# Second chunk's recurrence gates placed twelve matmuls earlier in a hybrid RG-LRU and attention encoder block

## The chip, the cores and the metric

The kernel runs on one core of a Trainium2 chip. The metric is the device time of one execution in microseconds (us). Before the change it was 1428.52 us, the median of three runs (1427.59 to 1429.19).

## What is computed

One encoder block over 1024 tokens of width 1024, all in float32. After an RMSNorm the block has two mixers side by side, a gated recurrence (RG-LRU) in both directions and a windowed attention; both are gated, added and projected, and a SwiGLU follows. The change lies in the recurrence:

```python
proj = rmsnorm(x, norm_mix_g) @ w_in
u, g_lru, q, k, v, z = jnp.split(proj, splits, axis=-1)
uc = centred_depthwise_conv(u, conv_w, conv_b)          # width 4
# for each direction, ub = uc in 16 blocks of 64 channels:
r = sigmoid(einsum("bshi,hij->bshj", ub, wa) + ba)
i = sigmoid(einsum("bshi,hij->bshj", ub, wx) + bx)
log_a = -8.0 * r * softplus(-lam)
a, beta = exp(log_a), sqrt(max(-expm1(2.0 * log_a), 0.0))
h = associative_scan(h[t] = a[t] * h[t-1] + beta[t] * (i * uc)[t])
y_a = (h_fwd + h_bwd) * gelu(g_lru)
merged = sigmoid(z_A) * y_a + sigmoid(z_B) * y_b
```

## The kernel before

**Layout.** Channels lie on the 128 partitions and tokens run along the free axis, so a tile of 128 channels is 128 x 1024. The recurrence is worked off in eight such chunks, numbered 0 to 7; the change touches chunk 1, the second.

**Products.** To keep float32 precision, each operand is split into a high part and a rest (`xh` and `xl`, `whi` and `wlo`), and a product is three matmuls per 128-deep step k: hi·hi, lo·hi, hi·lo. A projection of one chunk onto 1024 tokens has two halves (n = 0, 1) of 8 steps, so 48 matmuls of 512 columns. The projections go in a fixed list (`order`): for chunks from 2 on, u, then g (the GELU branch), then za (the gate z_A). `u` is accumulated in the PSUM tile `pu`, g and za in the two buffers of `pa`. The weight splits `whi` and `wlo` are made on GpSimd (lines 124 and 127), a ring of three ahead of the matmuls.

**A chunk of the recurrence** (`lru_chunk`) follows its u product:

- `evac_u` takes u out of PSUM and convolves it: two ScalarE passes (`uc`, line 610) and six VectorE passes (line 615).
- The result is split into `uh` (ScalarE, line 120) and `ul` (VectorE, line 127). These two are queued behind the next evacuation of g or za.
- The gate products `gp` follow, for direction d = 0 and then d = 1, twelve small matmuls each: four `gh` x `uh`, four `gh` x `ul`, four `gl` x `uh`. Each direction fills two PSUM tiles, and there are two buffers of these, so the gates of the second direction wait until ScalarE has read those of the first.
- ScalarE turns them into `r` and `i` (line 680, four passes of 64 x 1024), then `q` (tanh, line 689), `r` (exp, line 697) and `q` (sqrt, line 700), each once per direction. tanh and exp share a function table; GELU (line 624) and sqrt have others, and each switch is an ACT_TABLE_LOAD on ScalarE. The tanh of za (line 632) is a ScalarE pass too.
- VectorE does line 691 on `i`, the clamp of `q` (line 690), lines 703 and 704, the two scans (lines 706 and 708), the sum (709) and the output (713, 714).
- The gate weights of a chunk come in by four DMAs into `graw` (line 650) and are split into `gh` (ScalarE, line 120) and `gl` (GpSimd, line 127); a chunk's coroutine does that when it starts, for a later place in the stream.

**What sets the order.** TensorE's order is written by the program: coroutines are resumed by a counter (`clock`) that each matmul moves on by its columns times 0.00042, so a step k of three matmuls counts 0.645. `lru_chunk` yields a number, and its next part is written as soon as the counter has passed it. The first yield after the split stands between `uh`, `ul` and the gates of direction 0; the second (5.0 in chunk 1) between the two directions. The other engines' order is chosen by a list scheduler that follows the order in which instructions are written, within the priorities and `issue_after` ties given. Every engine then works off its own queue in that order.

Of the kernel before, what the change touches and what calls it, by code (L numbers as in the profile page):

```python
# [19 lines left out]
KD = D // P  # L20
# [11 lines left out]
def kernel(  # L32
# [36 lines left out]
    def kmtile(name, dt):  # L69
        return kmp.tile([P, S], dt, name=name, tag="km")  # L70
# [14 lines left out]
    def mm(o, lhsT, rhs, start, stop):  # L85
        pe.matmul(o, lhsT, rhs, start=start, stop=stop, skip_group_check=True)  # L86
        clock[0] += rhs.shape[-1] * 0.00042
# [30 lines left out]
    def to_hi(eng, o, i):  # L118
        if eng == "act":
            return act.activation(o, i, AF.Copy).ins  # L120
        elif eng == "dve":
            dve.tensor_copy(o, i)
        else:
            pool.tensor_scalar(out=o, in0=i, scalar1=1.0, scalar2=1.0, op0=ALU.mult, op1=ALU.mult)  # L124

    def to_lo(eng, o, i, hi):
        (dve if eng == "dve" else pool).tensor_tensor(out=o, in0=i, in1=hi.bitcast(F32), op=ALU.subtract)  # L127
# [99 lines left out]
    def gb(t, j, d, c):  # L227

        o = 88 + j * 16 + d * KD + c
        return pv[t * HD:(t + 1) * HD, o:o + 1]  # L230
# [409 lines left out]
    def lru_chunk(p2, psB, graw, c):  # L640

        def t2(tag, bufs=1, dt=F32):
            return p2.tile([P, S], dt, name=tag, tag=tag, bufs=bufs)

        for t, w in ((0, lru_wa), (1, lru_wx)):
            for j in range(2):
                o = slice(j * HD, (j + 1) * HD)
                dma(graw[o, :, t * HD:(t + 1) * HD], w[0, :, 2 * c + j].rearrange("d i o -> i d o"))  # L650
        gh = p2.tile([P, 2, P], F32R, name="gh", tag="gh", bufs=2)
        gl = p2.tile([P, 2, P], F32R, name="gl", tag="gl", bufs=2)
        to_hi("act", gh, graw)
        to_lo("pool", gl, graw, gh)
        uc = gs.pop(("uc", c))
        uh = t2("uh", 2, F32R)
        ul = kmtile("ul", F32R)
        before = last_evac[0]
        while last_evac[0] is before:
            yield 0.3  # L660
        with tc.high_priority(), tc.issue_after(last_evac[0]):
            to_hi("act", uh, uc)
            to_lo("dve", ul, uc, uh)
        yield {0: 3.5, 1: 11.0, KD - 1: 7.0}.get(c, 10.0)
        gate = {}
        for d in range(2):
            gp = [psB.tile([P, S], F32, name="gp", tag="gp", bufs=2) for _ in range(2)]
            for g, m, st, sp in ((gh, uh, True, False), (gh, ul, False, False), (gl, uh, False, True)):
                for n in range(2):
                    sl = slice(n * 512, (n + 1) * 512)  # L670
                    for j in range(2):
                        o = slice(j * HD, (j + 1) * HD)
                        mm(gp[j][:, sl], g[o, d, :], m[o, sl], st, sp)
                        clock[0] -= 0.1
            for t in range(2):
                r = t2("ri"[t], 3)
                i = slice(t * HD, (t + 1) * HD)
                for j in range(2):
                    o = slice(j * HD, (j + 1) * HD)
                    sig = act.activation(r[o, :], gp[j][i, :], AF.Tanh, bias=gb(t, j, d, c), scale=0.5).ins  # L680
                gate[t, d] = r
            if d == 0:
                yield {0: 6.0, 1: 5.0, KD - 1: 7.5}.get(c, 7.0)
        lru["gates"] += 1
        q = []
        for d in range(2):
            col = slice(d * KD + c, d * KD + c + 1)
            b = t2("q", 3)
            tanh = act.activation(b, gate[0, d], AF.Tanh, bias=sp2[:, col], scale=sp2[:, col]).ins
            dve.tensor_scalar(out=b, in0=b, scalar1=0.0, scalar2=None, op0=ALU.max)  # L690
            dve.scalar_tensor_tensor(out=gate[1, d], in0=gate[1, d], scalar=1.0, in1=uc, op0=ALU.add, op1=ALU.mult)
            q.append(b)
        with tc.high_priority(), tc.issue_after(sig), tc.issue_after(tanh):
            for d in range(2):
                a = gate[0, d]
                col = slice(d * KD + c, d * KD + c + 1)
                exp = act.activation(a, a, AF.Exp, bias=spm4[:, col], scale=spm4[:, col]).ins
        with tc.issue_after(exp):
            for d in range(2):
                act.activation(q[d], q[d], AF.Sqrt)  # L700
        for d in range(2):
            a, i = gate[0, d], gate[1, d]
            dve.scalar_tensor_tensor(out=q[d], in0=a, scalar=1.0, in1=q[d], op0=ALU.add, op1=ALU.mult)
            dve.tensor_tensor(out=i, in0=i, in1=q[d], op=ALU.mult)
            if d == 0:
                dve.tensor_tensor_scan(q[d], a, i, 0.0, ALU.mult, ALU.add)
            else:
                dve.tensor_tensor_scan(q[d][:, ::-1], a[:, ::-1], i[:, ::-1], 0.0, ALU.mult, ALU.add)
        dve.tensor_tensor(out=q[0], in0=q[0], in1=q[1], op=ALU.add)
        while ("ga", c) not in gs:  # L710
            yield 0.5
        g = gs.pop(("ga", c))
        dve.tensor_tensor(out=g, in0=g, in1=q[0], op=ALU.mult)
        dve.scalar_tensor_tensor(out=mB[c], in0=g, scalar=0.5, in1=mB[c], op0=ALU.mult, op1=ALU.add)
        lru["done"] += 1
# [6 lines left out]
    def mixers():  # L722
# [27 lines left out]
        def u_halves(c):  # L750
            ps = env[0][1].tile([P, S], F32, name="pu", tag="pu", bufs=1)
            for n in range(2):
                sl = slice(n * 512, (n + 1) * 512)
                yield from token_product(("u", c), sl, xh, xl, ps[:, sl])
            gs["u", c] = ps
            evac_u(c)
            spawn(lru_chunk(*env[0], c))
# [614 lines left out]
```

## Time and profile before

| | |
|---|---|
| runs | 1428.52 us median (1427.59 to 1429.19) |
| the profiled execution | 1428.95 us, of which its span is 1427.1 us |
| granted TensorE clock | 0.996 |
| TensorE (PE) busy | 1390.8 us, 97% of the span |
| VectorE (DVE) busy | 942.7 us, 66% |
| ScalarE (ACT) busy | 723.5 us, 51% |
| GpSimd (POOL) busy | 583.4 us, 41% |

In the views below, times are us from the start of the span. A timeline row gives start, duration, engine, line, operation, output and inputs, and in brackets the idle time of the engine just before and what ended it. A row with x4 is four instructions merged. A waits row gives the total, the number of times and the longest. In a table by windows, each engine has its busy time, and PEclk is the granted TensorE clock. The recurrence lies between 405 and 690 us.

### The profile page before, as it was taken

How to read it: one execution, taken by the hardware profiler on the slowest of the kernel's cores; microseconds unless marked ns; L12 is line 12 of the kernel's file. 1: busy time of each engine (PE TensorE's matmuls, PEld its weight loads, DVE VectorE, ACT ScalarE, POOL GpSimd, SP SyncE). 2: the span in 40 equal slices, each digit the busy share in tenths (PEclk: the TensorE clock that was granted, in tenths of full speed). 3: DMA queues.
4: the chain of work that ended last, by engine and by line, in shares of the span. 5: the costliest groups of instructions: out<-in, count | busy, mean ns of one | idle time of the engine just before them, and what ended most of it. 6: DMA issues, size and time to landing. Idle time of an engine off the chain costs nothing.

```text
span 1427.1 us, 18489 instructions
## 1 busy us (share of the span) xinstructions
PE 1390.8 (97%) x6606; PEld 1148.2 (80%) x6606; DVE 942.7 (66%) x1457; ACT 723.5 (51%) x1293; POOL 583.4 (41%) x522
## 2 busy tenths in 40 slices
PE   7999999999999899999999999999999999999997
PEld 6788888888887677777888878888888888888886
DVE  6357767677535898778967865444445454987886
ACT  6446556566528966669544533332333332544446
POOL 3434454454433425553454334555555562110002
PEclk9999999999999999999999999999999999999999
DMA  5111101110121111111253333333444435957643
GB/s 194 45 45 30 30 16 31 30 31 15 31 56 49 38 44 37 47 43 51 70 176 118 108 108 115 99 110 104 118 118 133 126 109 181 347 176 235 202 138 140
DMA packets 147548, 138.90 MB, mean 97 GB/s; under 512 B 11528, under 2 KB 117120, under 8 KB 147456
## 3 DMA queue, kind: packets, MB, share of 16 engines
q1 hardware_dynamic: 147456, 137.72, 31.1%
q8 instruction: 52, 0.85, 0.3%
q14 instruction: 40, 0.33, 0.1%
HBM read 119.08 MB, written 18.61 MB: 96 GB/s over the span
## 4 chain that ended last, share of the span: by engine, by line
PE 58%; ACT 3%; DVE 3%; issue 1%; DMA 0%; POOL 0%; ACTq 0%
PE wo L86 34%; PE pa L86 18%; PE pu L86 4%; PE gp L86 1%; PE wo L90 1%; DVE xg L855 0%; ACT i L680 0%; DVE wop L127 0%; DVE x L1273 0%; DMA wraw<-in_w_out_dram 0%; DVE ho L1186 0%; ACT x L1296 0%; ACT ho L1186 0%; ACT sg L1277 0%; DVE x L1293 0%
## 5 line engine op out<-in xcount | busy, mean ns | idle before, releaser
L86 PE MATMUL wo<-x,wop 128*128 128x512 f32 x1368 | 320.7, 390 | 2.1 <-DVE u L1042 1.1
L86 PEld LDWEIGHTS wo<-x,wop 128*128 128x128 f32 x1368 | 255.5, 188 | 56.2 <-ACT wop L998 2.7
L86 PE MATMUL pa<-xh,whi 128*128 128x512 f32 (+1 forms) x576 | 227.8, 395 | 1.5 <-ACT gg L624 1.4
L86 PE MATMUL pa<-xl,whi 128*128 128x512 f32 (+1 forms) x576 | 224.9, 390 | 0.9 <-DVE xl L253 0.7
L86 PE MATMUL pa<-xh,wlo 128*128 128x512 f32 (+1 forms) x576 | 223.8, 389 | 0.0
L127 POOL TENSOR_TENSOR wlo<-wraw,whi 128x1024 fp32r<-128x1024 f32 (+1 forms) x60 | 164.6, 2744 | 38.4 <-ACT whi L120 25.1
L86 PE MATMUL wo<-wo,ho 128*128 128x512 f32 x726 | 170.2, 389 | 0.0
L86 PEld LDWEIGHTS wo<-wo,ho 128*128 128x128 f32 x726 | 136.2, 188 | 28.7 <-DVE ho L1186 0.4
L124 POOL TENSOR_SCALAR whi<-wraw 128x1024 fp32r<-128x1024 f32 (+1 forms) x48 | 69.5, 1448 | 206.7 <-PE pa L86 147.9
L86 PEld LDWEIGHTS pa<-xh,wlo 128*128 128x128 f32 x576 | 108.3, 188 | 23.2
L86 PEld LDWEIGHTS pa<-xh,whi 128*128 128x128 f32 x576 | 108.5, 188 | 20.6 <-issue 3.5
L86 PEld LDWEIGHTS pa<-xl,whi 128*128 128x128 f32 x576 | 108.5, 188 | 16.6 <-DVE xl L253 2.1
L86 PE MATMUL pa<-x,wop 128*128 128x512 f32 x480 | 117.3, 391 | 0.0
L519 POOL TENSOR_SCALAR s<-s,es 128x384 f32<-128x384 f32 (+1 forms) x128 | 71.9, 581 | 97.2 <-DVE es L517 68.5
L579 DVE TENSOR_TENSOR pl<-pt,ph 128x384 fp32r<-128x384 f32 (+1 forms) x128 | 66.9, 522 | 60.6 <-ACT ph L578 58.0
L998 ACT ACTIVATE wop<-s 128x512 fp32r<-128x512 f32 x66 | 41.6, 630 | 128.7 <-POOL s L987 69.2
L86 PEld LDWEIGHTS pa<-x,wop 128*128 128x128 f32 x480 | 89.4, 188 | 18.2
L514 ACT ACTIVATE s<-s,nm 128x384 f32<-128x384 f32 (+1 forms) x128 | 74.0, 580 | 40.5 <-DVE nm L511 39.3
L578 ACT ACTIVATE ph<-pt 128x384 fp32r<-128x384 f32 (+1 forms) x128 | 58.6, 458 | 64.3 <-PE pt L90 49.7
L127 DVE TENSOR_TENSOR wop<-s,wop 128x512 fp32r<-128x512 f32 x66 | 53.5, 810 | 49.8 <-ACT wop L998 48.9
L505 DVE CUSTOM_DVE_ANT_0 s<-sp,bias 128x384 f32<-128x384 f32 (+1 forms) x128 | 66.3, 519 | 21.9 <-PE sp L86 20.6
L1279 POOL TENSOR_TENSOR x<-x,x 128x512 f32<-128x512 f32 x8 | 11.8, 1490 | 167.0 <-ACT sg L1277 167.0
(213 smaller groups left out, 2713.6 us busy)
## 6 DMA issues: line engine op xcount, KB each, us to landing
wraw<-in_w_in_dram SPq DMA_DIRECT2D x44, 512.0 KB, 4.0
wq<-in_w_ffn_out_dram SPq DMA_DIRECT2D x88, 256.0 KB, 3.7
wraw<-in_w_ffn_in_dram SPq DMA_DIRECT2D x26, 512.0 KB, 4.0
wup<-in_w_ffn_in_dram SPq DMA_DIRECT2D x22, 512.0 KB, 4.7
hid<-H SPq DMA_DIRECT2D x22, 512.0 KB, 3.2
h<-hid SPq DMA_DIRECT2D x44, 256.0 KB, 5.4
s<-in_w_ffn_out_dram SPq DMA_DIRECT2D x66, 128.0 KB, 2.2
wraw<-in_w_out_dram SPq DMA_DIRECT2D x16, 512.0 KB, 3.7
```

What stands on the lines that cost most here:

```text
L86: pe.matmul(o, lhsT, rhs, start=start, stop=stop, skip_group_check=True)
L90: pe.transpose(o, i, ident)
L124: pool.tensor_scalar(out=o, in0=i, scalar1=1.0, scalar2=1.0, op0=ALU.mult, op1=ALU.mult)
L127: (dve if eng == "dve" else pool).tensor_tensor(out=o, in0=i, in1=hi.bitcast(F32), op=ALU.subtract)
L505: dve.tensor_tensor_reduce(out=s[:, :n], in0=sp[:, :n], in1=bias[:, off:off + n], scale=1.0, scalar=-3.0e38, op0=ALU.add, op1=ALU.max, acc ...
L514: act.activation(s[:, :n], s[:, :n], AF.Exp, bias=nm[:, j:j + 1], accum_out=sm[:, j:j + 1])
L519: pool.tensor_scalar(out=s[:, :n], in0=s[:, :n], scalar1=es[:, j:j + 1], scalar2=1.0, op0=ALU.mult, op1=ALU.mult)
L578: act.activation(ph[:, o:o + n], pt[:, :n], AF.Copy)
L579: dve.tensor_tensor(out=pl[:, o:o + n], in0=pt[:, :n], in1=ph[:, o:o + n].bitcast(F32), op=ALU.subtract)
L998: act.activation(t[:, lo4], src, AF.Copy)
L1279: pool.tensor_tensor(out=x1[t][:, lo4], in0=x1[t][:, lo4], in1=gfin[:, lo4], op=ALU.mult)
```

## The change

In `lru_chunk` the first yield of chunk 1 becomes 9.0 instead of 11.0:

```diff
         with tc.high_priority(), tc.issue_after(last_evac[0]):
             to_hi("act", uh, uc)
             to_lo("dve", ul, uc, uh)
-        yield {0: 3.5, 1: 11.0, KD - 1: 7.0}.get(c, 10.0)
+        yield {0: 3.5, 1: 9.0, KD - 1: 7.0}.get(c, 10.0)
         gate = {}
         for d in range(2):
```

No instruction's work changes. Chunk 1's part of the program is written earlier, and so the order changes on five queues. On TensorE, in the product of chunk 2's u (`pu`), the gates of direction 0 of chunk 1 (`gp`) stand as follows (`xh_101` is step k = 6 of a half, `xh_102` step 7):

```order
 L86 MATMUL pu<-xl_109,whi 128x512
 L86 MATMUL pu<-xh_101,wlo 128x512
+L86 MATMUL gp<-uh,gh 128x512 x4
+L86 MATMUL gp<-ul,gh 128x512 x4
+L86 MATMUL gp<-uh,gl 128x512 x4
 L86 MATMUL pu<-xh_102,whi 128x512
 L86 MATMUL pu<-xl_110,whi 128x512
```

They stood behind step 2 of the second half and now stand behind step 6 of the first, four steps or twelve matmuls of 512 columns earlier. The gates of direction 1 move up by the same twelve, from behind step 2 of chunk 2's g to behind step 6 of the second half of its u.

On ScalarE, at the gates of chunk 1, the first two rows are direction 0, `uc` is the evacuation of chunk 2's u, and `gh` the split of a later chunk's gate weights:

```order
 L680 ACTIVATE r<-gp,pv 64x1024 x2
 L680 ACTIVATE i<-gp,pv 64x1024 x2
+L689 ACTIVATE q<-r,sp_86 128x1024
+L120 ACTIVATE gh<-graw 128x256
+L680 ACTIVATE r<-gp,pv 64x1024
 L610 ACTIVATE uc<-pu,pv 128x512 x2
-L689 ACTIVATE q<-r,sp_86 128x1024
-L120 ACTIVATE gh<-graw 128x256
-L680 ACTIVATE r<-gp,pv 64x1024 x2
-L680 ACTIVATE i<-gp,pv 64x1024 x2
+L680 ACTIVATE r<-gp,pv 64x1024
+L680 ACTIVATE i<-gp,pv 64x1024 x2
```

The evacuation of chunk 2's u now stands behind chunk 1's first tanh, the `gh` split and the first `r` of direction 1. Chunk 1's second tanh and its first exp, which the piece no longer shows, follow these rows and stand ahead of the GELU of chunk 2.

Further down ScalarE's queue come the second half of chunk 2's GELU (`gg`), chunk 1's second exp (`r`) and its sqrt (`q`), and chunk 2's za (`sA`):

```order
 L624 ACT_TABLE_LOAD
 L624 ACTIVATE gg<-pa 128x512
-L697 ACT_TABLE_LOAD
-L697 ACTIVATE r<-r,spm_87 128x1024
 L700 ACT_TABLE_LOAD
-L700 ACTIVATE q<-q 128x1024
+L700 ACTIVATE q<-q 128x1024 x2
 L632 ACT_TABLE_LOAD
 L632 ACTIVATE sA<-pa,hbg 128x512
-L700 ACT_TABLE_LOAD
-L700 ACTIVATE q<-q 128x1024
-L680 ACT_TABLE_LOAD
```

Three table loads go: one exp is ahead of the GELU and needs none, and the two sqrt stand together. The rows behind are the `r` and `i` of chunk 2.

On VectorE chunk 1's first clamp (690) moves ahead of chunk 2's convolution (615) and its second ahead of the last 691 and the split `ul`, and the pairs of 703 and 704 stand together. On GpSimd `gl` of a later chunk moves ahead of the weight split of chunk 3's u. On the DMA queue the four `graw` loads of the chunk after that move ahead of one `wraw` load.

## The prediction

> **What bounds the kernel now.** I read the page first, then the waits of TensorE in the stretch of the recurrence, then the timeline around each wait.
>
> ```profile
> span 1427.1 us, 18489 instructions
> PE 1390.8 (97%) x6606; PEld 1148.2 (80%) x6606; DVE 942.7 (66%) x1457; ACT 723.5 (51%) x1293; POOL 583.4 (41%) x522
> ```
>
> ```profile
> PE gp L86 <- ACT i L680: 6.2, 4, 4.4
> PE pa L86 <- ACT gg L624: 1.4, 1, 1.4
> ```
>
> TensorE is busy 97% of the span, so only what it waits for can be won. In the recurrence it waits twice for long: once for a GELU, once 4.4 us for the `i` passes. The timeline puts both in chunk 2, the chunk behind the one that is moved:
>
> ```profile
> 483.19 0.39 PE L86 MATMUL pa<-xh,wlo 128*128 128x512 f32 x1
> 485.02 0.50 PE L86 MATMUL pa<-xh,whi 128*128 128x512 f32 x1 [1.44 <-ACT gg L624]
> ...
> 494.90 0.39 PE L86 MATMUL pu<-xh,wlo 128*128 128x512 f32 x1
> 499.73 0.79 PE L86 MATMUL gp<-uh,gh 64*128 64x512 f32 x1 [4.44 <-ACT i L680]
> 500.86 1.22 PE L86 MATMUL gp<-uh,gh 64*128 64x512 f32 x3 [0.34 <-ACT i L680]
> 505.12 0.39 PE L86 MATMUL pu<-xh,whi 128*128 128x512 f32 x1
> ```
>
> The same passage without a wait is that of chunk 1's direction 0:
>
> ```profile
> 458.04 0.39 PE L86 MATMUL pu<-xh,whi 128*128 128x512 f32 x1
> 459.40 0.39 PE L86 MATMUL pu<-xh,whi 128*128 128x512 f32 x1
> 460.17 0.73 PE L86 MATMUL gp<-uh,gh 64*128 64x512 f32 x4
> 460.74 0.63 PE L86 MATMUL gp<-ul,gh 64*128 64x512 f32 x4
> 461.76 0.50 PE L86 MATMUL pu<-xh,whi 128*128 128x512 f32 x1
> 462.56 0.40 PE L86 MATMUL pu<-xh,whi 128*128 128x512 f32 x1
> 467.42 0.73 PE L86 MATMUL gp<-uh,gh 64*128 64x512 f32 x4
> ```
>
> A step of three matmuls takes (459.40 - 458.04) / 2 = 0.68 us, one matmul 0.23. From the last matmul before the gates (459.40 + 0.45 = 459.85) to the second step behind them (462.56) it is 2.71 us. In chunk 2 the same stretch, 494.90 to 505.12, takes 10.22: 7.5 us are lost there. About 5.5 of it is waiting. The rest is a slow restart: from 500.86 to 505.12 it is 4.26 us, where 2.39 less one matmul (2.25) is usual, so 2.0. The clock shows why:
>
> ```profile
> 485.10:494.40 9.30, 9.30 (x45) 7.18 (x46) 4.41 (x3) 9.18 (x9) 1.88 (x2) 1.00 0.01 3
> 499.70:506.00 6.30, 5.93 (x19) 4.00 (x20) 6.23 (x5) 5.25 (x6) 1.49 (x1) 0.57 0.19 56
> ```
>
> Behind the 4.44 us wait the granted clock (the third number from the end) was 0.57; behind the 1.44 us wait it stayed 1.00. The GELU wait cost 485.02 - 483.19 - 0.23 = 1.6. What could be won here is 7.5 + 1.6 = 9.1 us.
>
> **Term 1: the moved gates meet their own operand, +1.6 us.** Four steps earlier, direction 0 starts at 460.17 - 4 x 0.68 = 457.45, and its second group, the first that reads `ul`, 0.57 later at 458.02.
>
> ```profile
> 454.11 3.25 POOL L127 TENSOR_TENSOR wlo<-wraw,whi 128x1024 fp32r<-128x1024 f32 x1
> 455.02 3.42 DVE L703 SCALAR_TENSOR_TENSOR q<-r,q 128x1024 f32<-128x1024 f32 x1
> 458.37 1.21 DVE L127 TENSOR_TENSOR ul<-uc,uh 128x1024 fp32r<-128x1024 f32 x1
> ```
>
> `ul` is ready at 458.37 + 1.21 = 459.58, and nothing ahead of it moves. TensorE, which never waited there, now waits 1.6 us, and everything queued behind waits with it. So the move is 2.7 us on paper and 1.1 in effect. Bounds: 1.6, and 3.6 if the clock falls as after the 4.44 wait. I take 1.6, because the nearest row is the 1.44 wait with the clock at 1.00.
>
> `ul` is late because line 703 took 3.42 us beside GpSimd's `wlo`; it ended 1.1 us behind that one's end (457.36), as if it had waited for it. I use this below: of a GpSimd pass and a VectorE pass with two SBUF inputs, one holds up the other.
>
> **Term 2: chunk 2's two losses, -9.1 us, of which 0.3 stays.** ScalarE decides. Its rows before:
>
> ```profile
> 461.87 2.25 ACT L680 ACTIVATE r<-gp,pv 64x1024 f32<-64x1024 f32 x2 [4.26 <-PE gp L86]
> 464.14 2.25 ACT L680 ACTIVATE i<-gp,pv 64x1024 f32<-64x1024 f32 x2
> 466.42 1.45 ACT L610 ACTIVATE uc<-pu,pv 128x512 f32<-128x512 f32 x2
> 467.76 1.24 ACT L689 ACTIVATE q<-r,sp 128x1024 f32<-128x1024 f32 x1
> 478.30 1.06 ACT L120 ACTIVATE uh<-uc 128x1024 fp32r<-128x1024 f32 x1 [2.68 <-DVE uc L615]
> 484.37 0.60 ACT L624 ACTIVATE gg<-pa 128x512 f32<-128x512 f32 x1
> 494.29 1.28 ACT L680 ACT_TABLE_LOAD   x1
> 498.56 2.24 ACT L680 ACTIVATE i<-gp,pv 64x1024 f32<-64x1024 f32 x2
> ```
>
> I follow the new queue with these durations. Direction 0's `r` starts 2.7 - 1.6 = 1.1 earlier, at 460.8, and its four passes end at 465.3. TensorE reaches direction 1 at 467.42 - 2.72 + 1.6 = 466.3, so it does not wait there. Then tanh to 466.5. `gh` and the first `r` of direction 1 wait for TensorE (466.3 + 1.59 = 467.9); `r` ends about 469.4, `uc` 470.8 (467.87 before), the other `r` and two `i` 474.2, tanh 475.4, exp (as long) 476.7, a table load and a GELU half 478.6, a microsecond before TensorE wants its bank.
>
> Next is `uh`, which waits for chunk 2's convolution on VectorE:
>
> ```profile
> 474.24 4.03 DVE L615 SCALAR_TENSOR_TENSOR uc<-pu,pv,uc 128x510 f32<-128x510 f32 x6
> ```
>
> It can't start before 470.8. Chunk 1's clamp now stands ahead of it, and GpSimd's split of chunk 3's u weights, pushed behind `gl`, falls beside that: I put the start at 475.7, between 470.8 and 479.2 (one more GpSimd pair of 3.5 us, rows below), near the old 474.24. It ends at 479.7. `uh` 480.8; load, exp, load, GELU half (1.28 + 1.24 + 1.28 + 0.60) 485.2. TensorE wants that bank at 483.42 + 1.6 = 485.0, so some 0.3 us of wait stays instead of 1.6. Behind it: load, two sqrt (1.06 each, as `uh`), load, `sA` (0.6) to 490.5, then `r` and `i` of chunk 2, 4.5, to 495.0. TensorE wants direction 1 of chunk 2 at 495.13 - 1.6 + 1.6 + 0.3 = 495.4. The 4.44 us wait and its slow restart are gone, with 0.4 us to spare. Three loads less, 3.8 us, and one exp taken out from behind the second GELU half make most of the 5.8 us by which `i` ends sooner (500.80 before). The Trainium skill, "ScalarE: Activation LUTs", section "What ACT_TABLE_LOAD costs", gives 2.66 us for a switch, its drain counted; three would be 8.0, the 0.3 us would go and the sum would be 0.3 better. The trace disagrees: the load of 494.29 takes 1.28 and the queue goes on at once.
>
> **Term 3: VectorE has less slack in chunk 3, +1.2 us.**
>
> ```profile
> 489.93 1.22 DVE L703 SCALAR_TENSOR_TENSOR q<-r,q 128x1024 f32<-128x1024 f32 x1 [5.24 <-ACT q L700]
> 510.42 0.68 DVE L690 TENSOR_SCALAR q<-q 128x1024 f32<-128x1024 f32 x1
> 513.90 3.40 DVE L703 SCALAR_TENSOR_TENSOR q<-r,q 128x1024 f32<-128x1024 f32 x1 [2.80 <-ACT q L700]
> 526.55 3.41 DVE L127 TENSOR_TENSOR ul<-uc,uh 128x1024 fp32r<-128x1024 f32 x1
> ```
>
> ```profile
> 512.67 1.06 POOL L124 TENSOR_SCALAR whi<-wraw 128x1024 fp32r<-128x1024 f32 x1 [7.26 <-PE pu L86]
> 513.82 2.40 POOL L127 TENSOR_TENSOR wlo<-wraw,whi 128x1024 fp32r<-128x1024 f32 x1
> ```
>
> ```profile
> 530.31 0.63 PE L86 MATMUL gp<-ul,gh 64*128 64x512 f32 x4
> ```
>
> Chunk 3's `ul` ended at 529.96, only 0.35 before it was read. From 489.93 to 511.10 VectorE was busy or held up, 21.2 us. Now it starts there at 487.6 (sqrt done), 2.3 earlier, while TensorE is 7.2 earlier; and the GpSimd pair of 512.67 (3.5 us), released by TensorE, now falls into this stretch: 487.6 + 21.2 + 3.5 = 512.3. From 511.10 to 529.96 it was 18.9, of it 2.8 idle and twice 2.2 held up: 11.7 is left, so `ul` is ready near 524.0 to 524.3. TensorE wants it at 530.31 - 9.1 + 1.6 + 0.3 = 523.1. I take 1.2 us, between 0 (the pair finds a gap) and 3.6 (a second `wlo` gets ahead, 2.4).
>
> **What costs nothing.** `graw` goes ahead of one `wraw`:
>
> ```profile
> 472.12 1.25 SPq L650 DMA_DIRECT2D graw<-in_lru_wa_dram  x2
> ```
>
> ```profile
> wraw<-in_w_in_dram SPq DMA_DIRECT2D x44, 512.0 KB, 4.0
> ```
>
> Four issues of 0.63 behind `gl` (done near 469.4) let `wraw` go at 472 and land at 476; its split waits for the end of chunk 2's g, about 479.6. If that cover were gone, each us late is one of chunk 3's g weights, wanted 25 us later. The pair that `gl` now precedes is wanted at 492.5 and ends near 475.
>
> **The sum.** -9.1 + 1.6 + 0.3 + 1.2 = -6.0 us. The profiled execution took 1428.95 us (span 1427.1, 1.9 around it), so 1422.9; it lies 0.4 above the median of 1428.52, so the median should be 1422.5. Behind chunk 3 nothing is moved, and TensorE simply runs 6 us earlier. What a measurement of this kernel can tell from no change is about 0.2%, 2.9 us.
>
> **The rivals.**
> *New waits eat the gain (0.09).* Term 3 is at its worse end of 3.6, the clock falls there as behind the 4.44 wait (2.0), and term 2 keeps 2.0: -9.1 + 1.6 + 2.0 + 3.6 + 2.0 = +0.1, 1428.6. For it: VectorE is full from 489.93 on. Against: both terms must come out near their worse ends.
> *The change does little (0.05).* The gates can't pass `ul`; if ScalarE's new order saved nothing and only the 1.1 us went through, both waits shrink by 1.1 and 1.6 is added: 1428.5 - 2.2 + 1.6 = 1427.9. Against: the three loads are gone from the queue.
> *Slower (0.08).* Chunk 2's convolution is held behind two GpSimd pairs, since `uc` is now evacuated 3 us later and the weight split later too. Both GELU halves and chunk 2's gates are queued behind `uh`. Each us that the convolution ends after 479.7 is a us of TensorE's wait for the GELU half; with a wait like the 4.44 one the clock falls too (2.0). It loses all at a delay of 4.0 (4.0 + 2.0 + 0.3 + 1.6 + 1.2 = 9.1); with 6.9 for two pairs the time is 1422.5 + 6.9 + 2.0 = 1431.4. Against: one of the pairs is over by 475. The point at which the clock falls lies between waits of 1.44 and 4.44 in this trace. The Trainium skill, "TensorE: Matmul & The Clock Gate", section "What's actually happening", puts it at an idle window of about 3.4 us; by that this rival's break-even has its 2.0, and rival one's 3.6 as well.
>
> **Chances.** Forecast 0.78, the rivals 0.09, 0.05 and 0.08. The forecast is faster by over 0.2%, the first two rivals are no change, the third is slower. Range: with terms 2 and 3 at nothing, 9.1 - 1.6 = 7.5 are won, 1421.0, and half a us is added for the spread of the runs. With term 2 at its worse end (0.3 + 3.5 of wait) 9.1 - 1.6 - 3.8 - 1.2 = 2.5 are won, 1426.0; with term 3 at its worse end 3.6, 1424.9. The forecast alone would leave out 0.22, so the range reaches on to the second rival: 1420.5 to 1428.0.
>
> **What would show it.** Right: a new TensorE wait of `gp` for VectorE's `ul` near 458 of about 1.5 us at clock 1.00; no wait of 4 us for `i` near 495; at most half a us for the GELU near 485; a wait of 0 to 3.6 for `ul` near 523. Wrong: a convolution of chunk 2 that starts after 479, or any wait over 3 us in the recurrence.

## The result, and the profile after

With the change the kernel takes 1421.05 us (median of four runs, 1420.54 to 1421.23), beside 1428.05 for the kernel before in its four runs. The two medians give a ratio of 0.9951; the ratio on record is 0.9945, with a 95% interval of 0.9932 to 0.9958, and the ratios further down are those on record too. The forecast was 1422.5, faster by 6.0; by the medians it is faster by 7.0.

The span and busy lines of the page after. Against before the span is 7.8 us shorter, TensorE is busy 2.3 us less, and ScalarE has three instructions less:

```profile
span 1419.3 us, 18488 instructions
PE 1388.5 (98%) x6606; PEld 1147.9 (81%) x6606; DVE 939.4 (66%) x1457; ACT 720.1 (51%) x1290; POOL 584.3 (41%) x522
```

TensorE's waits of the change in the stretch of the recurrence (total, times, longest). The GELU line is gone, the 4.4 us wait for `i` too, and `ul` is new; the two small waits for `i` that are left are in chunk 7, where before had them as well:

```profile
PE gp L86 <- DVE ul L127: 2.2, 2, 1.4
PE gp L86 <- ACT i L680: 1.4, 2, 0.8
```

The two waits for `ul` on the change's TensorE timeline, in chunk 1 (459.06) and chunk 3 (523.15), and between them direction 1 of chunk 2 (494.67), where before waited 4.44 us and came back at a granted clock of 0.57:

```profile
456.90 0.73 PE L86 MATMUL gp<-uh,gh 64*128 64x512 f32 x4
459.06 0.73 PE L86 MATMUL gp<-ul,gh 64*128 64x512 f32 x4 [1.43 <-DVE ul L127]
...
460.18 0.50 PE L86 MATMUL pu<-xh,whi 128*128 128x512 f32 x1
...
494.67 0.73 PE L86 MATMUL gp<-uh,gh 64*128 64x512 f32 x4
...
521.64 0.73 PE L86 MATMUL gp<-uh,gh 64*128 64x512 f32 x4
523.15 0.73 PE L86 MATMUL gp<-ul,gh 64*128 64x512 f32 x4 [0.78 <-DVE ul L127]
```

The theory of the cause is read off one queue, and E5 tests it. ScalarE in the change, from the split `uh` of chunk 2 on:

```profile
478.63 1.06 ACT L120 ACTIVATE uh<-uc 128x1024 fp32r<-128x1024 f32 x1 [0.85 <-DVE uc L615]
483.57 0.60 ACT L624 ACTIVATE gg<-pa 128x512 f32<-128x512 f32 x1
484.19 1.28 ACT L700 ACT_TABLE_LOAD   x1
485.48 2.01 ACT L700 ACTIVATE q<-q 128x1024 f32<-128x1024 f32 x2
489.39 2.24 ACT L680 ACTIVATE r<-gp,pv 64x1024 f32<-64x1024 f32 x2
491.65 2.25 ACT L680 ACTIVATE i<-gp,pv 64x1024 f32<-64x1024 f32 x2
```

The same stretch of ScalarE before, with the passes that the change takes out of it:

```profile
479.27 1.23 ACT L689 ACTIVATE q<-r,sp 128x1024 f32<-128x1024 f32 x1
480.51 1.28 ACT L697 ACT_TABLE_LOAD   x1
481.81 1.25 ACT L697 ACTIVATE r<-r,spm 128x1024 f32<-128x1024 f32 x1
...
491.92 1.28 ACT L700 ACT_TABLE_LOAD   x1
493.21 1.06 ACT L700 ACTIVATE q<-q 128x1024 f32<-128x1024 f32 x1
...
497.85 0.69 ACT L632 ACTIVATE sA<-pa,hbg 128x512 f32<-128x512 f32 x1
```

From the end of `uh` to the end of `i` it was 500.80 - 479.36 = 21.4 us before and is 493.90 - 479.69 = 14.2 in the change. The 7.2 us are three table loads that are gone (3.8), one exp (1.2) and one tanh (1.2) that are now done while ScalarE used to wait for the convolution, and half of `sA` (0.7) that now comes behind `i`: 7.0 before rounding, and a rest of 0.2. (The third load is that of 494.29, shown in the prediction.)

**How far a single time can be trusted.** I measure each version by its stretch as well: from the first gates of chunk 0 to direction 1 of chunk 7, on TensorE. Before:

```profile
426.63 0.73 PE L86 MATMUL gp<-uh,gh 64*128 64x512 f32 x4
...
671.30 0.49 PE L86 MATMUL gp<-uh,gh 64*128 64x512 f32 x1 [0.77 <-ACT i L680]
```

The change:

```profile
426.06 0.74 PE L86 MATMUL gp<-uh,gh 64*128 64x512 f32 x4
...
664.25 0.50 PE L86 MATMUL gp<-uh,gh 64*128 64x512 f32 x1 [0.77 <-ACT i L680]
```

That is 244.67 and 238.19 us, a difference of 6.48. What lies outside the stretch (the execution's time less the stretch) is 1184.28 and 1182.87. A stretch is that of the one profiled execution, a median that of all executions. One of E2's nine executions took 4950.94 us and is left out of E2's ratio.

### The profile page after: what moved, and what is told of

It reads as the page before. It is cut to its first block, busy times and chain, and to the rows that moved or that the text cites. A ratio compares the mean times of both kernels' runs of the same rounds, so it can differ in the third digit from the quotient of the medians.

```text
span 1419.3 us, 18488 instructions
## 1 busy us (share of the span) xinstructions
PE 1388.5 (98%) x6606; PEld 1147.9 (81%) x6606; DVE 939.4 (66%) x1457; ACT 720.1 (51%) x1290; POOL 584.3 (41%) x522
## 4 chain that ended last, share of the span: by engine, by line
PE 81%; DVE 10%; ACT 6%; issue 2%; DMA 1%; POOL 0%; SPq 0%; ACTq 0%; DVEq 0%
PE wo L86 34%; PE pa L86 32%; PE pu L86 4%; PE yp L86 3%; PE sp L86 2%; PE pt L90 2%; PE gp L86 1%; DVE q L703 1%; DVE uc L615 1%; PE wo L90 1%; DVE pl L579 1%; ACT s L514 1%; DVE i L691 0%; DVE q L706 0%; DVE i L704 0%
```

## The experiments

The theory: ScalarE's order pays (one exp and one tanh ahead of chunk 2's GELU, three table loads less), and the moved gates as such only cost, by the wait for `ul`. The rival: the gates' place pays, that is, `r` and `i` of chunk 1 come sooner and all that hangs on them too. Two smaller questions are what a table load costs and whether the wait for `ul` in chunk 3 lies on the path.

Each version ran beside the kernel before, whose median was 1429.09 us beside E1 to E4, 1428.29 beside E5 to E8 and 1428.69 beside E9 to E12. "Steps" are how many steps of three matmuls direction 0 and direction 1 of chunk 1's gates stand sooner than before. Stretch and time are us less (-) or more (+) than before.

| | version | steps | stretch | time | ratio (95%) |
|---|---|---|---|---|---|
| | the change | 4, 4 | -6.48 | -7.0 | 0.9945 (0.9932 to 0.9958) |
| E1 | direction 1 one step | 0, 1 | -5.56 | -5.3 | 0.9960 (0.9947 to 0.9972) |
| E2 | direction 0 alone | 4, 1 | -4.75 | -3.4 | 0.9972 (0.9962 to 0.9982) |
| E3 | direction 1 three steps | 0, 3 | -7.14 | -8.0 | 0.9944 (0.9932 to 0.9957) |
| E4 | one step further | 5, 5 | -4.92 | -5.3 | 0.9968 (0.9956 to 0.9980) |
| E5 | the change, old ScalarE order | 4, 4 | +2.04 | +2.1 | 1.0011 (1.0002 to 1.0020) |
| E6 | two steps | 2, 3 | -6.73 | -7.4 | 0.9946 (0.9934 to 0.9959) |
| E7 | two steps, chunk 2 later | 2, 3 | -6.75 | -6.7 | 0.9947 (0.9935 to 0.9960) |
| E8 | the change again | 4, 4 | -6.47 | -6.6 | 0.9949 (0.9935 to 0.9962) |
| E9 | square roots apart | 4, 4 | -3.16 | -4.3 | 0.9969 (0.9958 to 0.9980) |
| E10 | `ul` read last | 4, 4 | -6.21 | -5.9 | 0.9957 (0.9944 to 0.9969) |
| E11 | E3, chunk 3 two steps later | 0, 3 | -8.18 | -8.8 | 0.9936 (0.9923 to 0.9948) |
| E12 | one step, chunk 3 two steps later | 1, 3 | -8.05 | -8.3 | 0.9941 (0.9927 to 0.9955) |

In the expectations of E1 to E4, E6 and E7 "chunk 2's gates" are those of the moved chunk, which is chunk 1 in this document; the time named with each wait says which one is meant. In that of E8, "chunk 1's first gates" are chunk 0's here. In E2 direction 1 did not quite stay: it came out one step sooner, as in E1.

### E1: direction 1 one step sooner

```diff
-                yield {0: 6.0, 1: 5.0, KD - 1: 7.5}.get(c, 7.0)
+                yield {0: 6.0, 1: 4.4, KD - 1: 7.5}.get(c, 7.0)
```

> Only direction 1 of chunk 2's gates moves, by one step of three matmuls (0.68 us) sooner; direction 0 stays where it was, so no wait for its own low half. ScalarE then has the exp ahead of the GELU in chunk 2, one table load fewer and the square roots still apart. Theory A (it is ScalarE's order that pays, not where the gates stand): the GELU wait of 1.4 us near 485 is gone, the wait for the second input gate near 495 is still there but about 3.5 us instead of 4.4; 1.4 + 0.9 = 2.3 us below before if TensorE still comes back at the lower clock, 4.3 us if it does not (the restart was 2.0). Theory B (it is direction 0's gates being sooner that pays): direction 0 has not moved, so the two waits stay and the time is before's within 1 us.

A single step of direction 1 wins 5.56 of the change's 6.48 us, with direction 0 where it was. The order on ScalarE turned: the second tanh and the first exp now stand ahead of the GELU. The GELU wait is gone, and the long wait, in E1's TensorE timeline, is 1.88 instead of 4.44:

```profile
494.53 0.50 PE L86 MATMUL gp<-uh,gh 64*128 64x512 f32 x1 [1.88 <-ACT i L680]
495.66 0.72 PE L86 MATMUL gp<-uh,gh 64*128 64x512 f32 x3 [0.64 <-ACT i L680]
```

This speaks for the theory and against the rival, and the gain is larger than I had put for the theory (2.3 to 4.3). I had counted the load that goes and too little for what is taken out from behind `uh`, which is a tanh, an exp and a load, 1.23 + 1.25 + 1.28 = 3.8 us. The profiled execution is a favourable one, though: it and one more had a granted clock of 0.999 and took 1421.5 and 1422.0 us, the other three had 0.995 to 0.998 and took 1423.8 to 1424.8. E2 is split in the same way, with 1422.5 and 1423.1 at 0.999 and 1424.9 to 1427.5 at 0.995 to 0.997. By the medians E1 wins 5.3 of some 7.

### E2: direction 0 alone

```diff
-        yield {0: 3.5, 1: 11.0, KD - 1: 7.0}.get(c, 10.0)
+        yield {0: 3.5, 1: 9.0, KD - 1: 7.0}.get(c, 10.0)
...
-                yield {0: 6.0, 1: 5.0, KD - 1: 7.5}.get(c, 7.0)
+                yield {0: 6.0, 1: 7.0, KD - 1: 7.5}.get(c, 7.0)
```

> Only direction 0 of chunk 2's gates moves, by four steps as in the change; direction 1 stays where it was. ScalarE has the exp ahead of the GELU, but the square roots are not paired: one load fewer than before, not three. Theory A (ScalarE's order pays): the wait for the low half near 458 is the change's own, 1.4 us; no GELU wait; the second input gate ends two loads and more later than in the change, near 497, so TensorE waits 1.5 to 2.5 us near 495, at clock 1.00 if that is short enough: 5.0 us below before. Theory B (direction 0's place pays): as the change, 7.0 us below.

From chunk 2's `uh` on, ScalarE's order is that of E1, and direction 0 stands four steps sooner. The waits are 1.45 us for `ul` and 1.55 + 0.64 for `i`; the stretch is 0.8 us worse than E1's. Direction 0's place is not what pays.

### E3: direction 1 alone, three steps

```diff
-                yield {0: 6.0, 1: 5.0, KD - 1: 7.5}.get(c, 7.0)
+                yield {0: 6.0, 1: 3.0, KD - 1: 7.5}.get(c, 7.0)
```

> Only direction 1 of chunk 2's gates moves, three steps (2.0 us) sooner; direction 0 stays. ScalarE's order in chunk 2 is the change's in full (exp ahead of the GELU, square roots paired, three loads fewer). Theory A (ScalarE's order pays): no wait for the low half in chunk 2, both of chunk 3's waits gone as in the change, and in their place direction 1 of chunk 2 waits about 1.0 us for the input gate of direction 0: 7.0 to 7.7 us below before, level with the change or a little better. Theory B (direction 0's place pays): within 2 us of before.

The passes and loads from chunk 1's second tanh to chunk 2's `i` stand as in the change, and direction 0 is untouched. I had expected the change's order in full; it differs in that the evacuation `uc` stands ahead of chunk 1's first tanh, as before, and a `gh` split stands elsewhere. The stretch is 0.7 us better than the change's. E3's TensorE waits in the recurrence show why: no wait for `ul` in chunk 1 (the one left, 0.7, is chunk 3's), and 0.56 more for `i`:

```profile
PE gp L86 <- ACT i L680: 2.0, 3, 0.8
PE gp L86 <- DVE ul L127: 0.7, 1, 0.7
```

The theory holds: the gain is had without moving direction 0 at all.

### E4: one step further

```diff
-        yield {0: 3.5, 1: 11.0, KD - 1: 7.0}.get(c, 10.0)
+        yield {0: 3.5, 1: 8.0, KD - 1: 7.0}.get(c, 10.0)
```

> The change carried one step (0.68 us) further: both directions' gates of chunk 2 stand 5 steps sooner than before instead of 4. ScalarE's order in chunk 3's stretch is the change's. Theory A (ScalarE's order pays, the move itself only costs): the wait for the low half near 458 grows from 1.4 to 2.1 us, nothing else moves: 6.3 us below before, 0.7 slower than the change. Theory B (the sooner the better): 7.5 us or more below before.

The wait for `ul` is 2.12 us, as expected, but 1.6 us of the stretch are lost against the change, not 0.7. E4's timeline and, under it, a window of it (length, PE busy with its count, granted clock, DMA share, GB/s) show that the clock fell:

```profile
459.31 1.22 PE L86 MATMUL gp<-ul,gh 64*128 64x512 f32 x4 [2.12 <-DVE ul L127]
460.33 1.06 PE L86 MATMUL gp<-uh,gl 64*128 64x512 f32 x4
```

```profile
459.20:462.90 3.70, 3.59 (x12) 0.55 0.30 89
```

The step costs 0.7 and the slow stretch some 1.5, and 0.6 comes back in chunk 3, whose wait for `ul` is 0.17 instead of 0.78.

### E5: the gates of the change, ScalarE in the old order

The ties hold chunk 1's second tanh behind chunk 2's `uh`, its second exp behind the second GELU half and its second sqrt behind the first half of `sA` (`nxt()` yields until the next evacuation is written). For it the loops over the exps and square roots are written with the ties inside, and the splits `uh` are recorded in `gs`; the gates are not touched. Ahead of chunk 2's first GELU half ScalarE keeps the change's order, so "old" means from there on.

```diff
+            if (c, d) == (1, 1):
+                while ("uh", 2) not in gs:
+                    yield 0.1
+            with tc.issue_after(gs["uh", 2]) if (c, d) == (1, 1) else nullcontext():
+                tanh = act.activation(b, gate[0, d], AF.Tanh, ...).ins
...
+            if (c, d) == (1, 1):
+                yield from nxt()
+                exp = last_evac[0]
```

> All of the gates stand where the change puts them (four steps sooner, direction 1 eight steps behind direction 0); ScalarE's queue is held in before's order from chunk 2's GELU on (GELU and the high half ahead of the exps, each exp and square root apart, three table loads more than in the change). The computation is the same. Theory A (the gain is ScalarE's order): the change's wait for the low half near 458 stays at 1.4 us, and the wait for the second input gate near 495 comes back at 1.5 to 3.5 us, less than before's 4.4 because direction 1's sigmoids end 1.5 us sooner, with the restart of up to 2 us where it is over 2 us; GELU wait 0 to 0.5. In all 2 to 5.5 us below before, so 1.5 to 5 us above the change. Theory B (the gain is the gates' place): level with the change, 7.0 us below before.

This is the run that decides. With the gates where the change has them and the old order on ScalarE, the kernel is slower than before by 2.1 us, 2.04 by the stretch. E5's TensorE timeline:

```profile
458.34 0.73 PE L86 MATMUL gp<-ul,gh 64*128 64x512 f32 x4 [1.45 <-DVE ul L127]
...
484.63 0.50 PE L86 MATMUL pa<-xh,whi 128*128 128x512 f32 x1 [0.57 <-ACT gg L624]
...
499.33 0.50 PE L86 MATMUL gp<-uh,gh 64*128 64x512 f32 x1 [4.44 <-ACT i L680]
500.47 1.22 PE L86 MATMUL gp<-uh,gh 64*128 64x512 f32 x3 [0.63 <-ACT i L680]
```

The wait for `ul` is paid, the 4.44 us wait is back to the hundredth, and only the GELU wait is shorter. That the long wait is the same is no accident: in both versions the second GELU half releases TensorE last, and from that half's start to the end of `i` ScalarE takes the same time, 500.80 - 484.37 = 16.43 us before and 500.42 - 483.98 = 16.44 here. All 8.5 us between E5 and the change are ScalarE's order, with what follows from it on VectorE, whose queue is the change's until chunk 2's convolution is done. I had left the theory 2 to 5.5 us of gain here, since direction 1's sigmoids end sooner; that was wrong. ScalarE waits at `uh` for chunk 2's convolution all the same:

```profile
467.92 1.43 ACT L610 ACTIVATE uc<-pu,pv 128x512 f32<-128x512 f32 x2
477.91 1.06 ACT L120 ACTIVATE uh<-uc 128x1024 fp32r<-128x1024 f32 x1 [3.25 <-DVE uc L615]
```

Counted from chunk 0's gates (425.33), `uc` is evacuated at 42.6 instead of 39.8 and `uh` starts at 52.6 instead of 51.7. So the sooner gates delay what the long chain really hangs on, by 0.9 us. With the 1.1 us by which the restart behind the long wait is slower than before (last section), that is E5's 2.0.

### E6 and E7: two steps, and a gate further on

```diff
-        yield {0: 3.5, 1: 11.0, KD - 1: 7.0}.get(c, 10.0)
+        yield {0: 3.5, 1: 10.0, KD - 1: 7.0}.get(c, 10.0)
...
-                yield {0: 6.0, 1: 5.0, KD - 1: 7.5}.get(c, 7.0)
+                yield {0: 6.0, 1: 4.2, KD - 1: 7.5}.get(c, 7.0)
```

> Direction 0 of chunk 2's gates moves two steps (1.36 us) instead of four, direction 1 three steps instead of four; ScalarE's order is the change's. Theory A (the order pays, the move costs only what it goes beyond the low half's slack of 1.16 us): wait for the low half near 458 0.2 us instead of 1.4, no wait of direction 1 for the input gate of over 0.4 us, nothing near 485 and 495; chunk 3's wait of 0.8 us stays: 1.5 us below the change, 8.5 below before. Theory B (the sooner the better): 3.5 us below before, half of the change's gain.

The wait for `ul` in chunk 1 is down to the expected 0.2 us (the second group starts 0.81 behind the first instead of 0.57), but of the 1.3 us that this saves only 0.25 shows in the stretch. E6's waits in the recurrence say where the rest went:

```profile
PE gp L86 <- DVE ul L127: 1.0, 1, 1.0
PE pa L86 <- ACT gg L624: 0.5, 1, 0.5
```

TensorE now comes 1.2 us sooner to the GELU, and neither ScalarE nor, behind it, VectorE is sooner by as much: the GELU wait returns with 0.5, and chunk 3's wait for `ul` grows from 0.8 to 1.0. E7 adds `2: 10.6` to the first table and `2: 6.4` to the second:

> The version with two steps, and direction 0 of chunk 3's gates one step (0.68 us) later, direction 1 where it was. If chunk 3's wait for the low half (0.78 us, 0.94 with the slower matmuls behind it) is on TensorE's path like chunk 2's, 0.7 us go: 9.2 us below before, 0.7 below the version with two steps. If what waits there is hidden by a later wait, level with that version.

The expectation doesn't fit the edit. Key 2 is chunk 2, and the wait near 522 is chunk 3's, so the edit left it alone (0.99 us), and the stretch is E6's. E7 says nothing on its question; E11 does.

### E8: the change again

> The change itself once more, for how far one execution differs from another outside the recurrence. If the 0.6 us before the first gates and the 0.8 us behind the last ones are spread of single executions, this profile shows other values there, and the stretch from chunk 1's first gates to chunk 3's second direction is 105.9 us again. If they come from the change, they are 0.6 and 0.8 again. The time 7.0 us below before either way, within 0.7.

The stretch is 238.20 us, as in the first profile to a hundredth, and the part outside it 1421.68 - 238.20 = 1183.5, where it had been 1182.9. Over all the profiled executions it goes from 1182.1 (E11) to 1185.1 (E10). Part of that is the clock: in E4, E5, E7, E8 and E10 it fell to half for 3.4 us right behind the stretch, and from the stretch's end on these took 757.9 to 758.0 us, all others 756.8 to 757.7. The change and E8 are one kernel, and one has this fall and the other not; the last section shows the rows. So the 1.4 us by which before's profiled execution is longer outside the stretch are within the spread of single executions, and what the change does is in the stretch.

### E9: square roots apart

```diff
+            if (c, d) == (1, 1):
+                for _ in range(3):
+                    seen = last_evac[0]
+                    while last_evac[0] is seen:
+                        yield 0.1
+                exp = last_evac[0]
             with tc.issue_after(exp):
                 act.activation(q[d], q[d], AF.Sqrt)
```

> The change with one thing undone on ScalarE: chunk 1's two square roots stand apart again, the second behind the first half of chunk 2's sA, with the two table loads (1.28 us each) that this takes. The first exp stays ahead of the GELU and the gates stand where the change has them. Theory A (ScalarE's order pays, and the loads by their own time): the GELU wait near 485 stays away, the i passes of chunk 2 end 2.6 to 3.2 us later than in the change, of which 0.8 are spare: TensorE waits 1.8 to 2.4 us near 495, 4.4 to 5.2 us below before, and 2 less if the clock falls. If a load cost twice as much as its row shows, the wait would be 4.4 to 5 and the clock would fall: level with before. Theory B (the gates' place pays): 7.0 below before.

The edit lets three evacuations pass, so that chunk 1's second square root comes behind the first half of chunk 2's `sA`. This one undoing costs half the gain: 3.3 us of the stretch. E9's ScalarE rows at the second sqrt and the end of `i`:

```profile
489.62 1.28 ACT L706 ACT_TABLE_LOAD   x1
490.92 1.06 ACT L706 ACTIVATE q<-q 128x1024 f32<-128x1024 f32 x1
492.00 1.28 ACT L680 ACT_TABLE_LOAD   x1
493.29 2.25 ACT L680 ACTIVATE r<-gp,pv 64x1024 f32<-64x1024 f32 x2
...
497.42 1.11 ACT L680 ACTIVATE i<-gp,pv 64x1024 f32<-64x1024 f32 x1
```

Counted from chunk 0's gates, `i` ends at 498.53 - 427.14 = 71.4 instead of 67.8: 3.55 us later, which is two loads (2.56), half of `sA` (0.69), 0.1 for the sqrts that no longer overlap, and 0.2. So a load costs its 1.28 us on this queue. The Trainium skill, "ScalarE: Activation LUTs", section "What ACT_TABLE_LOAD costs", counts a drain of 1.38 us with each; as an estimate from that figure, two loads would have made it 6.3, which the trace doesn't show. TensorE's wait came in two pieces, 0.91 and 1.35, and the clock fell for 3.4 us behind them, so the cost is 3.3.

### E10: `ul` read last

```diff
-            for g, m, st, sp in ((gh, uh, True, False), (gh, ul, False, False), (gl, uh, False, True)):
+            for g, m, st, sp in ((gh, uh, True, False), (gl, uh, False, False), (gh, ul, False, True)):
```

> The change with the three groups of a gate's product in another order, in all chunks: the high half with gh, the high half with gl, then the low half, so that ul is read 0.47 us later. If the wait for the low half is what the moved gates cost, the two waits of 1.4 and 0.8 us shrink by 0.47 each and the time is 0.9 us below the change, 7.9 below before. If VectorE's chain to the low half is itself started by TensorE and nothing is won, level with the change.

A miss: 0.3 us worse than the change by the stretch. Chunk 3's wait shrank as expected, from 0.78 to 0.29. Chunk 1's did not (1.48), because `gh` and with it GpSimd's `gl` came forward. E10's VectorE row, then its GpSimd row:

```profile
458.90 1.75 DVE L127 TENSOR_TENSOR ul<-uc,uh 128x1024 fp32r<-128x1024 f32 x1
```

```profile
458.53 1.03 POOL L127 TENSOR_TENSOR gl<-graw,gh 128x256 fp32r<-128x256 f32 x1 [0.64 <-ACT gh L120]
```

Beside that pass `ul` took 1.75 us, not 1.21, and the half microsecond was gone. Also new is a wait of 1.52 for `i` in chunk 7, 0.77 in the change. That wait is where the gain went: TensorE came to it 0.48 us sooner than in the change, counted from chunk 0's gates, and was released 0.27 later, which is what the stretch is worse by.

### E11 and E12: chunk 3's gates later

E11 is E3 with chunk 3's direction 0 two steps later, and E12 the same with direction 0 of chunk 1 one step sooner (10.4 and 3.6 for chunk 1):

```diff
-        yield {0: 3.5, 1: 11.0, KD - 1: 7.0}.get(c, 10.0)
+        yield {0: 3.5, 1: 11.0, 3: 11.2, KD - 1: 7.0}.get(c, 10.0)
...
-                yield {0: 6.0, 1: 5.0, KD - 1: 7.5}.get(c, 7.0)
+                yield {0: 6.0, 1: 3.0, 3: 5.8, KD - 1: 7.5}.get(c, 7.0)
```

> Direction 0 of chunk 1's gates where before has it, direction 1 three steps sooner (as the version with direction 1 alone), and direction 0 of chunk 3's gates two steps (1.36 us) later, its direction 1 in place. If chunk 3's wait for its low half (0.74 us, 0.9 with what follows) is on TensorE's path, it goes and the time is 0.9 us below the version with direction 1 alone, 9 below before. If not, level with that version.

> Direction 0 of chunk 1's gates one step sooner than before (0.68 us, inside the low half's slack of 1.16), direction 1 three steps, so six behind direction 0; chunk 3's direction 0 two steps later. No wait for a low half in chunk 1 or 3, less of the wait of direction 1 for the input gate than the 1.2 us that the version with direction 1 alone shows there; a GELU wait of up to 0.5 us near 483 may come back as in the version with two steps. 0 to 0.7 us below the version with direction 0 in place, 9 to 9.7 below before.

In E11 the wait for `ul` in chunk 3 is gone, and the stretch is 1.0 us shorter than E3's: that wait was on the path. At 1419.90 us it has the lowest median and the shortest stretch, 1.7 us below the change by the stretch (1.2 and 1.8 below its two medians, with intervals that overlap). In E12 the wait for `i` in chunk 1 is gone as well, but the GELU wait of 0.52 returned as in E6, and it is level with E11.

## Where the prediction was right, and the step that failed

**What bounds it.** Right. The 9.1 us of chunk 2's two losses are what the change could win, and they are gone.

**Term 1, +1.6.** Right. From the gates' first row to the product behind them it is 460.18 - 456.90 = 3.28 us instead of 1.59: +1.69, at clock 1.00. E3 shows that this price isn't needed for the gain.

**Term 2, -9.1 + 0.3.** The mechanism was right, and E5 shows it as ScalarE's order alone; the 0.3 was too much. In the change there is no GELU wait. The second GELU half ended at 484.17, forecast 485.2; 0.6 of this is that chunk 0's gates already stood 0.6 sooner in this execution, and by the other 0.5 the chain ran ahead of the forecast.

This is the step that failed: the start of chunk 2's convolution, which the forecast put at 475.7, a choice between two bounds, and from which it kept 0.3 us of GELU wait. It started at 474.57, or 475.14 if the 0.57 of the execution's own is added. What it names as the cause is there: the clamp ahead of the convolution took 2.89 us beside GpSimd's `wlo`, where without such a pass it takes 0.68. VectorE's rows in the change, then GpSimd's:

```profile
471.76 2.89 DVE L690 TENSOR_SCALAR q<-q 128x1024 f32<-128x1024 f32 x1
474.57 4.03 DVE L615 SCALAR_TENSOR_TENSOR uc<-pu,pv,uc 128x510 f32<-128x510 f32 x6
```

```profile
470.85 3.25 POOL L127 TENSOR_TENSOR wlo<-wraw,whi 128x1024 fp32r<-128x1024 f32 x1
```

The forecast's rule named VectorE passes with two SBUF inputs alone; the clamp has one and was held up too. Its account of why `i` ends sooner also left out the tanh (1.23) taken out from behind `uh`, though its times had it.

**Term 3, +1.2.** Right in kind, and the other term that was sized wrong: 523.15 - 521.64 = 1.51 instead of 0.57, so +0.94. `ul` was ready at 523.09, forecast 524.0 to 524.3, again with 0.6 of it the execution's own. E11 shows that it lay on the path.

**The sum.** -9.1 + 1.69 + 0 + 0.94 = -6.47, and the stretch shows -6.48; an agreement this close is partly luck, since the 9.1 is rounded. The forecast of -6.0 was off by half a microsecond, 0.3 in term 2 and 0.26 in term 3, less 0.09 in term 1. Of the 1.45 us between 1422.5 and 1421.05, this is 0.5; another 0.5 is that before's median, 1428.52 in three runs, is 1428.05 in four; the rest lies outside the stretch, where E8 shows a spread of this size, and its cause is open in part. So half a microsecond of the 7.0 is not shown to be the change's.

**The rivals.** "The change does little" had the waits shrink by 1.1 us each if ScalarE's order saved nothing, for 1427.9. E5 is that case, and it is worse: the long wait did not shrink at all, because both its ends hang on the convolution, by way of `uh` and the GELU half, and not on the sigmoids. The slower rival had that piece right (a later `uc`), but in the change the passes taken out from behind `uh` cover it: `uh` waits 0.85 us where it waited 2.68. "Behind chunk 3 nothing is moved" held: the second directions of chunk 3 and of chunk 7 come 7.04 and 7.05 us sooner.

**The clock.** I had the point at which it falls between waits of 1.44 and 4.44, and used 2.0 us as the price. That frame was wrong; the last section has what the runs show.

## What to carry to other kernels

A number that places work on one engine can pay through the order that it brings about on another: the gates' new place cost 1.7 us, and ScalarE's new order was worth 8.5. Before such a number is tuned, the question is which order is wanted, and then which place brings that order about without passing an operand: here direction 1 alone did it, and direction 0 could stay. And when a large wait goes, the engine that waited arrives sooner everywhere behind it, so the next waits (`ul` in chunk 3, the GELU at two steps) are worth a look of their own.

## What the runs showed of the hardware

**The clock does not fall at a certain length of wait.** One wait of 1.43 us (the change) and two of 1.88 and 0.64 (E1) left it at 1.00. One of 2.12 (E4) and two of 0.91 and 1.35 (E9) brought it to half. Windows of E1 over its two waits and behind them (length, PE busy with its count, granted clock, DMA share, GB/s):

```profile
492.60:496.00 3.40, 0.89 (x5) 1.00 0.01 3
496.00:502.00 6.00, 6.00 (x32) 1.00 0.36 102
```

And of before: here the clock fell in the middle of the wait, 2.9 us after it began, and stayed at 0.50 until 505.1:

```profile
495.30:498.20 2.90, 0.00 (x0) 1.00 0.00 0
498.20:504.80 6.60, 4.73 (x15) 0.50 0.28 79
```

It stayed low for 3.41 us in E4 and E9, and for twice that, 6.83, in before and E5, whose wait was the same 4.44 but where the fall came only at 500.2, when TensorE was already back. So the price of such a wait is a matter of when it falls, not of its length alone: the second 4.44 us wait cost 1.1 us more than the first in what followed it.

The clock falls and comes back on a beat of its own. In E4 it fell at 459.15 and again at 667.36, 208.21 us or 61 times 3.413 later; in E5 at 500.19 and 674.27, 174.08 us or 51 times. Where the beat lies differs between executions of one kernel, and with it what the same waits cost. In chunk 7 the change and E8 have the same two waits, 0.77 and 0.63. In E8 both lie in one window of the beat, and the clock fell at its end (TensorE, then windows as above, with all five engines' busy times):

```profile
663.70 0.50 PE L86 MATMUL gp<-uh,gh 64*128 64x512 f32 x1 [0.77 <-ACT i L680]
```

```profile
662.97:666.38 3.41, 2.04 (x12) 1.23 (x12) 3.41 (x3) 3.33 (x4) 3.33 (x2) 1.00 0.00 0
666.38:669.79 3.41, 3.41 (x9) 2.69 (x9) 3.41 (x2) 3.36 (x4) 1.77 (x1) 0.50 0.14 29
```

In the change an edge of the beat (664.32, 190 steps of 3.413 from 15.79, where the clock first came up in that execution) falls between the two waits, and the clock stayed up:

```profile
664.32:667.74 3.42, 2.79 (x15) 1.85 (x16) 3.42 (x2) 3.37 (x4) 3.34 (x2) 1.00 0.00 0
```

The Trainium skill, "TensorE: Matmul & The Clock Gate", section "What's actually happening", has a free-running window of about 3.4 us, and a fall after at least one idle window. The beat agrees with the first; that a whole window must be idle does not hold here: in E8's window TensorE was busy for 2.04 us of 3.41. What share decides is open. Idle time alone does not: E2's window from 663.08 to 666.49 had as much of it as E8's, 1.37 us, and E1's from 490.88 to 494.29 had 1.64, and both kept the clock. So that the edge between the change's two waits kept its clock up is likely, but not shown. Part of the spread of the times comes from this beat, as E8's longer time behind the stretch shows; how much, no run here shows.

**A short GpSimd pass delays a VectorE pass too.** `gl`, 128 x 256 and 1.03 us, was enough to stretch `ul` from 1.21 to 1.75 us (E10). A pass with one input can be held up as well: the clamp, 2.89 us beside `wlo` instead of 0.68.
